# Memory query projection of a decoder step: from full products on column thirds to seven half-size products per pair of feature tiles

## The chip, the core and the metric

The kernel runs on one core of one Trainium2 chip. The metric is the time of one execution on the device, in microseconds (us); lower is better. The profile is that of one execution. Engines are named as in the profile: PE is TensorE's matmul, PEld its weight load, DVE is VectorE, ACT is ScalarE, POOL is GpSimd, SP is SyncE, which here issues DMAs.

## What is computed

One layer of a decoder for 1024 prompt tokens and 8 sample tokens, all in float32, with an output projection, attention into 256 memory tokens and an MLP. The part that matters here, from the reference:

```python
xp = xp + merge_groups(oa, o_r, gr, ...) @ w_out[l]
mk_p, mv_p = mem_kv(mem_prompt, norm_mem_kv[l], w_mk[l], w_mv[l])
xp = xp + mem_attend(rmsnorm(xp, norm_mem_q[l]), mk_p, mv_p, w_mq[l], w_mo[l])
xp = xp + sq_relu_mlp(rmsnorm(xp, norm_mlp[l]), w_up[l], w_down[l])

def mem_attend(h, mk, mv, w_mq, w_mo):
    q = (h @ w_mq).reshape(B, T, H_M, DH_M)          # 1024 x 1024 weights, 4 heads of 256
    s = jnp.einsum('bthd,bmhd->bhtm', q, mk) * DH_M ** -0.5
    p = jax.nn.softmax(s, axis=-1)
    o = jnp.einsum('bhtm,bmhd->bthd', p, mv).reshape(B, T, D_MODEL)
    return o @ w_mo
```

`rmsnorm` multiplies a token's row by one factor, `rsqrt(mean(x*x) + eps)`, and each feature by a gain. The sample tokens go through the same projections and attend to cached memory keys and values (`cmk`, `cmv`).

## The kernel before

Activations are kept transposed: 8 feature tiles of 128 partitions, with T = 1032 token columns (1024 prompt, 8 sample). CH is a third of them (344), HALF is 516, QC is 258. Each float32 operand of a large product is split into a high part of type fp32r (a copy on ACT) and the rest (a subtraction on DVE); a product is then three matmuls per 128-row step: high x high, high x low, low x high. `UH` and `UL` hold the two parts of the right operand, the rings `wh` and `wl` (4 buffers each) those of the weights, and `raw` (3 buffers) the weights as loaded.

The order of instructions comes from a planner that puts each engine's instructions in the order in which they would be ready by its own estimate, the earlier in the program first. Three things override it: `pin[0] = True` holds matmuls in program order, `tc.issue_after(ins)` puts a block's instructions behind `ins` on its engine, and `behind("Activation", "DVE")` does so for the latest instruction of both engines. Every engine, and SP's DMA queue, then runs its list strictly in order. A tile's tag names a buffer that tiles of the same tag share; a new tile waits until an older one is released.

The stages around the change:

1. Output projection (`proj_residual`, matmuls `pr_o`): per feature tile `ft` and column third `c`, first thirds 0 and 1 of all tiles, then third 2. `store` adds the residual into the tiles `x2[ft]`, squares them on ACT and adds the squares on POOL. `rstd_bcast` sums the squares by matmuls (`rs`), sends the row to a column and back through DRAM (power on POOL in `rsqrt_small`) and broadcasts it into `rb2`. Then eight DMAs write `x2` to `X2` in DRAM.
2. `split_gain` (L131) multiplies `x2` by the gain and splits it into `UH`/`UL`, columns 0 to 687 first, then the last third.
3. Query projection (`mq`, L1632 to L1661): for each of 4 pairs of feature tiles, 2 tiles x 3 thirds, each one accumulation of 8 x 3 matmuls of 344 columns. The eviction (L1652) multiplies by `rb2` and -1/16 into `qm`; its 8 sample columns go to `qdm` (POOL). After pairs 1 and 3, `dec_scores` replicates the sample queries (`rep_rows`) and multiplies them with the cached keys, loaded as `cmk` in 512 KB pieces: three of four on DVE (L1625), every fourth on POOL with a DVE reduction (L1619, L1620). The operands of the memory tokens (`mh`, `ml`) and their norm factor are prepared at the head of this stage.
4. Memory keys and values: `mem_keys_now(0)` (`mk`), two blocks of `mv`, `mem_keys_now(1)`, outputs to DRAM and back for `head_kv(0)`.
5. Attention: a pinned loop of 16 turns (4 heads x 4 token blocks). Turn by turn `scores` (`ms`, minimum L1764, exponential with scale -1 L1768, reciprocal, multiplication), `weights` (transposes, split), `values` (`mpv`, L1803/L1804 into `UH`/`UL`). `head_q` splits a head's queries, its low part on POOL (L1747). The rest of `mk` fills the gaps.
6. The memory output projection (`pr_m`), the up projection (L2106) and the down projection (L2271). The latter two already use the seven-product scheme with 258-column matmuls.

Of the kernel before, what the change touches and what calls it, by code (L numbers as in the profile page):

```python
# [19 lines left out]
P = 128  # L20
D = 1024
# [27 lines left out]
def decoder_step(ctx: ExitStack, tc: tile.TileContext, i: dict, o: dict):  # L49
# [764 lines left out]
    def dec_softmax(A, dt, SC, nt, c, nm):  # L814
# [7 lines left out]
        m3 = A.tile([P, 8, 16], F32, tag="dex", name=f"dm3_{nm}", bufs=2)[:c]  # L822
# [14 lines left out]
    def rep_rows(A, dt, src, nf, dst, nm, b0=0):  # L837

        for b in range(b0, b0 + nf // 4):
            tp = dt(f"rep_{nm}_{b}")  # L840
            for x in range(4):
                ex = A.tile([P, 8, 16], F32, tag="dex", name=f"dex_{nm}_{b}_{x}", bufs=2)
                nc.vector.tensor_copy(ex, src[:, 4 * b + x, :].unsqueeze(2).to_broadcast([P, 8, 16]))
                nc.tensor.transpose(tp[:, x * P : x * P + P], ex.rearrange("p s g -> p (s g)"), ident)
# [556 lines left out]
    def proj_residual(A, bank, base, ktorder, xsrc, xdst, ssum, nm, us0, steps, when, parts, ahead=0, early=None, stage=()):  # L1401
# [16 lines left out]
        def store(ps, ft, c):  # L1418
# [54 lines left out]
    def rstd_bcast(A, PS, bufs, ssum, last, r, dst, nm, rtag):  # L1473
# [9 lines left out]
        col = A.tile([86, 12], F32, tag="rcol", name=f"rcol_{nm}")  # L1483
        nc.sync.dma_start(col, row)
        rc = A.tile([86, 12], F32, tag="rrc", name=f"rrc_{nm}")
        rsqrt_small(rc, col, 12, 1.0 / D, 86)
        nc.sync.dma_start(rrow[r : r + 1, :].rearrange("a (p c) -> p (a c)", p=86), rc)
        nc.sync.dma_start(dst, bcast_rows(rrow[r : r + 1, :], P, T))

    with pool("x2") as XP:  # L1490
        x2 = [XP.tile([P, T], F32, tag=f"x2_{ft}", name=f"x2_{ft}") for ft in range(8)]
        g_mq = XP.tile([P, 8], F32, tag="g_mq", name="g_mq")
        nc.sync.dma_start(g_mq, i["g_mq"])
        with pool("c") as A:
            def decode_values():
                def dt(name):
                    return PB.tile([P, 512], F32, tag="av", name=name, bufs=1)

                acc = A.tile([P, T], F32, tag="dacc", name="dacc")
                for k in range(8):  # L1500
                    raw = A.tile([P, 1024], F32, tag="draw", name=f"cv_{k}", bufs=4)
                    gather(raw, i["cache_v"], idx, k)
                    with tc.issue_after(seen["DVE"]):
                        for x in range(8):
                            c = slice(x * P, x * P + P)
                            w = at[:, x % 4, 2 * k + x // 4 : 2 * k + x // 4 + 1]
                            if k == 0:
                                nc.vector.tensor_scalar(acc[:, c], raw[:, c], w, None, ALU.mult)
                            else:
                                nc.vector.scalar_tensor_tensor(acc[:, c], raw[:, c], w, acc[:, c], ALU.mult, ALU.add)  # L1510
                    yield
                vp = dt("vrep")
                mm(vp, selg, vdec, True, True)
                pd = A.tile([P, 1024], F32, tag="draw", name="pdv_8", bufs=4)
                nc.vector.tensor_mul(
                    pd[:, :512].rearrange("p (a v) -> p a v", v=P), vp.rearrange("p (a v) -> p a v", v=P),
                    at[:, :, 16:17].to_broadcast([P, 4, P]),
                )
                nc.vector.tensor_add(acc[:, :512], acc[:, :512], pd[:, :512])
                yield  # L1520

                with tc.issue_after(seen["PE"]):
                    op = dt("dop")
                    mm(op[:8, :], selgt, acc[:, 0:512], True, False)
# [44 lines left out]
    with pool("d") as A:  # L1569
# [62 lines left out]
        for pr in range(4):  # L1632
# [6 lines left out]
            for f, c in late + rest if pr else rest + late:  # L1639
# [15 lines left out]
                if (f, c) == (1, 2) and pr % 2:  # L1655
                    for _ in dec:
                        pass
# [932 lines left out]
```

## Time and profile before

| | |
|---|---|
| median of 3 runs | 1518.12 us (1514.62 to 1518.33) |
| the profiled execution | 1516.72 us, its span 1515.0 us |
| granted TensorE clock | 0.996 |
| PE busy | 1483.5 us (98%) |
| DVE, ACT, POOL busy | 1121.2 us (74%), 669.3 us (44%), 423.6 us (28%) |
| HBM | 150 GB/s over the span |

A matmul's recorded duration covers its way through the array, so records of neighbours overlap; the pace of matmuls is read from starts or from the merged chain. Records on DVE overlap a little too. A line number can be that of a helper: L75 is `mm`, L118 the low half in `unit_of`, L134 the low half in `split_gain`.

### The profile page before, as it was taken

The numbers are of one execution on the slowest core, as the hardware profiler recorded it, in microseconds if no ns is written. First come the engines' busy times: TensorE is split into PE (matmuls) and PEld (weight loads), VectorE is DVE, ScalarE is ACT, GpSimd is POOL, SyncE is SP. The second block draws the span as 40 slices with busy tenths as digits, with TensorE's granted clock in tenths as the row PEclk, the third lists the DMA queues.
The fourth block names the chain that finished last, engine by engine and source line by source line (L and its number), as shares of the span: only waits on it lengthen the run. The fifth ranks groups of instructions, "written<-read, shape, count | busy, mean of one in ns | idle before, by whom it ended". The sixth has DMA issues, their size and how long they took to land.

```text
span 1515.0 us, 27770 instructions
## 1 busy us (share of the span) xinstructions
PE 1483.5 (98%) x10909; PEld 1406.3 (93%) x10909; DVE 1121.2 (74%) x2200; ACT 669.3 (44%) x1314; POOL 423.6 (28%) x441
## 2 busy tenths in 40 slices
PE   9999999999999999999999999999999999999997
PEld 7899779998669999989999999999999999999997
DVE  7656536888766735557786988888889889787885
ACT  7433435666552432047535633333334444333454
POOL 0035323124313321125132223443335202020360
PEclk9999999999999999999999999999999999999999
DMA  8155727214847157362492433343335784536213
GB/s 292 56 186 187 185 58 186 70 35 138 248 140 268 56 194 191 120 200 86 152 323 71 145 129 134 140 154 140 141 142 169 258 285 125 183 86 193 87 43 112
DMA packets 120860, 231.39 MB, mean 153 GB/s; under 512 B 13216, under 2 KB 72661, under 8 KB 120602
## 3 DMA queue, kind: packets, MB, share of 16 engines
q1 hardware_dynamic: 89008, 170.50, 35.4%
q0 software_dynamic: 20592, 39.53, 8.4%
q10 hardware_dynamic: 11130, 19.60, 3.4%
q8 instruction: 85, 1.39, 0.4%
q14 instruction: 45, 0.37, 0.1%
HBM read 170.24 MB, written 57.52 MB: 150 GB/s over the span
## 4 chain that ended last, share of the span: by engine, by line
PE 77%; DVE 11%; DMA 5%; issue 3%; ACT 3%; POOL 1%; SPq 0%; DVEq 0%; ACTq 0%; POOLq 0%
PE dn L2271 17%; PE Z L2106 7%; PE qkp L75 6%; PE pr_o L75 6%; PE mq L75 5%; PE Y L2106 5%; PE pr_m L75 4%; PE X L2106 4%; PE grp L75 3%; PE sp L75 2%; PE av L75 2%; DVE wu L1921 1%; PE mpv L75 1%; DMA raw_up<-in_wall 1%; PE vap_z L511 1%
## 5 line engine op out<-in xcount | busy, mean ns | idle before, releaser
L2271 PE MATMUL dn<-UH,wd 128*128 128x258 f32 x1792 | 324.5, 283 | 1.8 <-DVE c L2375 1.3
L2271 PEld LDWEIGHTS dn<-UH,wd 128*128 128x128 f32 x1792 | 277.4, 189 | 2.5 <-ACT wd L2249 0.8
L2271 PE MATMUL dn<-UL,wd 128*128 128x258 f32 x896 | 252.8, 282 | 0.0
L2271 PEld LDWEIGHTS dn<-UL,wd 128*128 128x128 f32 x896 | 169.0, 189 | 0.0
L2132 ACT ACTIVATE hq<-r 128x258 f32<-128x258 f32 x128 | 53.7, 420 | 161.5 <-DVE r L2131 161.5
L2375 DVE TENSOR_TENSOR c<-c,dn 128x258 f32<-128x258 f32 x216 | 88.4, 418 | 32.6 <-PE dn L2271 31.1
L2106 PE MATMUL Z<-T_h,wu 128*128 128x258 f32 x512 | 99.8, 286 | 4.7 <-DVE u L2160 3.3
L1921 DVE TENSOR_TENSOR wu<-raw_up,wu 128x512 fp32r<-128x512 f32 x96 | 93.1, 971 | 9.7 <-ACT wu L1920 9.6
L2106 PE MATMUL X<-UH,wu 128*128 128x258 f32 x512 | 97.5, 282 | 0.0
L2249 ACT CAST wd<-raw_d 128x512 fp32r<-128x512 f32 x96 | 58.6, 618 | 77.1 <-PE dn L2271 72.2
L2106 PEld LDWEIGHTS Z<-T_h,wu 128*128 128x128 f32 x512 | 81.6, 189 | 6.4 <-DVE u L2160 4.1
L2242 ACT CAST UH<-raw_h 128x1032 fp32r<-128x1032 f32 x56 | 58.7, 1055 | 58.1 <-PE dn L2271 27.7
L2250 DVE TENSOR_TENSOR wd<-raw_d,wd 128x512 fp32r<-128x512 f32 x96 | 75.2, 789 | 11.5 <-ACT wd L2249 11.3
L2243 DVE TENSOR_TENSOR UL<-raw_h,UH 128x1032 fp32r<-128x1032 f32 x56 | 76.8, 1371 | 9.0 <-ACT UH L2242 8.9
L2106 PEld LDWEIGHTS X<-UH,wu 128*128 128x128 f32 x512 | 81.3, 188 | 0.2 <-ACT p L2157 0.2
L2139 POOL TENSOR_TENSOR ht<-hq 128x258 f32<-128x258 f32 x31 | 20.6, 663 | 195.6 <-ACT hq L2132 195.3
L117 ACT CAST wh_u<-raw_u 128x1024 fp32r<-128x1024 f32 x43 | 44.4, 1047 | 64.8 <-PE mq L75 42.9
L2263 POOL TENSOR_TENSOR raw_d<-raw_d,raw_d 128x512 f32<-128x512 f32 x16 | 22.1, 1378 | 181.0 <-DVE raw_d L2259 130.3
L2106 PE MATMUL Z<-T_l,wu 128*128 128x258 f32 x256 | 72.5, 283 | 0.0
L2106 PE MATMUL X<-UL,wu 128*128 128x258 f32 x256 | 72.2, 282 | 0.0
L1920 ACT CAST wu<-raw_up 128x512 fp32r<-128x512 f32 x96 | 57.2, 611 | 27.2 <-DVE raw_up L1927 24.1
L118 DVE TENSOR_TENSOR wl_u<-raw_u,wh_u 128x1024 fp32r<-128x1024 f32 x39 | 49.5, 1277 | 19.0 <-ACT wh_u L117 18.9
(595 smaller groups left out, 4808.9 us busy)
## 6 DMA issues: line engine op xcount, KB each, us to landing
raw_u<-in_wall SPq DMA_DIRECT2D x49, 512.0 KB
HT<-ht POOLq DMA_DIRECT2D x32, 516.0 KB
raw_h<-HT SPq DMA_DIRECT2D x32, 516.0 KB
raw_up<-in_wall SPq DMA_DIRECT2D x32, 512.0 KB
raw_d<-in_wall SPq DMA_DIRECT2D x32, 512.0 KB
HQ<-hq ACTq DMA_DIRECT2D x32, 387.0 KB
raw_h<-HQ SPq DMA_DIRECT2D x24, 516.0 KB
cmk<-in_cmk SPq DMA_DIRECT2D x16, 512.0 KB
```

Of the source, the lines that this page charges most:

```text
L75: pinned(nc.tensor.matmul(out, l, r, start=start, stop=stop))
L118: (lo_engine or nc.vector).tensor_sub(wl[:, :n], raw[:, :n], wh[:, :n].bitcast(F32))
L1920: nc.scalar.copy(w[:, :512], src)
L1921: nc.vector.tensor_sub(w[:, 512:], src, w[:, :512].bitcast(F32))
L2106: pinned(nc.tensor.matmul(ps, l, r[:, k, :], start=first and k == 0 and x == 0, stop=k == 3 and x == 2, skip_group_check=True))
L2132: nc.scalar.activation(h[:, PLACE[quad], :], r, AF.Square)
L2242: nc.scalar.copy(h, rv)
L2243: nc.vector.tensor_sub(l, rv, h.bitcast(F32))
L2249: nc.scalar.copy(w[:, :512], src)
L2250: nc.vector.tensor_sub(w[:, 512:], src, w[:, :512].bitcast(F32))
L2271: pinned(nc.tensor.matmul(ps, l, r[:, k, cq], start=first and k == 0 and x == 0, stop=k == 3 and x == 2, skip_group_check=True))
L2375: nc.vector.tensor_add(y, y, ps)
```

## The change

- **The product.** The 1024 x 1024 weights are seen as four pairs of 128-column tiles, and the features and the tokens are halved: a 2 x 2 by 2 x 2 block product, done with seven products of half size (numbered 1 to 7) and sums of blocks before and after. Products 1 and 2 (`first_columns`) run for pairs 0 and 1, then for pairs 2 and 3; then `other_columns` does products 6, 5, 7, 4, 3 of one pair after the other (6, 7, 4, 5, 3 for pair 0). All matmuls of the stage are pinned and have 258 columns. The weights are stored tile by tile (`_unit128`); each unit is loaded twice, once for products 1 and 2 (`WA`) and once for the sums (`q_loads`, `q_operands`).
- **The right operands.** Only the first half of the columns is split by `split_gain`. `early_sums`, `late_sums` and `last_sums` form the sums of `x2` blocks in place and split them into `T3`, `UH` and `UL`. `X2` is therefore written from inside `store`, in two pieces per feature tile, and third 2 of the output projection runs in the order 0, 4, 1, 5, 2, 6, 3, 7.
- **The norm factor.** Evictions are plain copies (ACT) and additions (DVE). The factor, as a column per token block (`fq`, through DRAM), becomes the scale of the exponential, and the maximum is multiplied by `nfq` for its bias. `rb2` is used for the sample columns alone.
- **Around it.** The `cmk` rows are loaded in 32 pieces of 256 KB into the tags `mph`/`mpl`, with bufs 2 each, which the `p1` tiles use too; all are reduced on DVE. The first half runs in pairs 2 and 3, the second in the `mv` stage. The loads of the memory tokens move to pairs 2 and 3. `x2`'s buffers stay alive through attention and hold `head_q`'s tiles; `head_q` of heads 2 and 3 is put behind the latest `mph` copy on ACT.

```diff
 # proj_residual
+            if c:
+                xs = slice(0, 2 * CH) if c == 1 else cs
+                nc.sync.dma_start(X2[ft, :, xs], xdst(ft)[:, xs])
-        order = [(ft, c) for ft in range(8) for c in range(2)] + [(ft, 2) for ft in range(8)]
+        order = [(ft, c) for ft in range(8) for c in range(2)] + [(ft, 2) for ft in KT_PAIRS]
...
-        for lo, hi in ((0, 2 * CH), (2 * CH, T)):
-            for kt in range(8):
-                split_gain(x2[kt][:, lo:hi], g_mq, kt, lo, hi)
+    for kt in range(8):
+        split_gain(x2[kt][:, :HALF], g_mq, kt, 0, HALF)
...
         def dec_scores(half):
...
+            for n in range(18):
+                if n < 16:
+                    raws[n] = A.tile([P, HALF], F32, tag=("mph", "mpl")[n % 2], name=f"cmk_{half}_{n}", bufs=2)
+                    nc.sync.dma_start(raws[n][:, :512], i["cmk"][:, n, ch])
+                if n < 2:
+                    continue
+                k = n - 2
+                with seq():
+                    for x in range(2):
+                        nc.vector.tensor_tensor_reduce(...)
                 yield
...
+        def early_sums(k):
+            x, z = x2[k], x2[k + 4]
+            nc.scalar.activation(x[:, hi_t], x[:, hi_t], AF.Copy, scale=g1)
+            nc.vector.scalar_tensor_tensor(x[:, lo_t], x[:, lo_t], g1, x[:, hi_t], ALU.mult, ALU.subtract)
+            nc.vector.scalar_tensor_tensor(x[:, hi_t], z[:, hi_t], g2, x[:, hi_t], ALU.mult, ALU.subtract)
+            nc.scalar.copy(T3[0][:, k, :], x[:, hi_t])
+            nc.vector.tensor_sub(T3[1][:, k, :], x[:, hi_t], T3[0][:, k, :].bitcast(F32))
...
+        def q_product(kind, pr, q, c, w, first):
+            if first:
+                banks_q[kind, pr, c] = PS.tile([P, 512], F32, tag="acc", name=f"mq_{kind}_{pr}_{c}", bufs=6)[:, :QC]
+            for k in range(4):
+                for x, (l, r) in enumerate(((wk, rh), (wk, rl), (wkl, rh))):
+                    pinned(nc.tensor.matmul(ps, l, r[:, k0 + k, tk], ...))
...
+        def q_operands(pr):
+            with seq():
+                nc.vector.tensor_sub(s3, a11, a21)
+            yield
+            # likewise: a21 += a22; a11 = a21 - a11; split 6, 7, 5, 4; a12 -= a11 and split 3
...
+        def other_columns(pr, order):
+            for n, q in enumerate(order):
+                for c in range(2):
+                    ps = q_product("z" if q in (6, 7, 4) else "y", pr, q, c, WB[pr][q], q in (6, 5))
+                    with seq():
+                        if q == 6:
+                            nc.vector.tensor_add(u2[:, cq], ps, p1[pr][:, cq])
+                        elif q == 7:
+                            nc.vector.tensor_add(u3[:, cq], ps, p1[pr][:, cq])
+                            if c in y5:
+                                nc.vector.tensor_add(f1[:, ch], y5[c], u3[:, cq])
+                        elif q == 4:
+                            nc.vector.tensor_add(f1[:, cq], ps, p1[pr][:, cq])
+                        elif q == 3:
+                            nc.vector.tensor_add(f0[:, ch], ps, u2[:, cq])
...
+                    yield
...
+        for k in range(3):
+            early_sums(k)
+        WA = {pr: unit(U_MQ + 2 * pr) for pr in range(4)}
+        with tc.issue_after(seen["rs"]):
+            early_sums(3)
+        q_loads(0)
+        late = late_sums()
+        next(late)
+        first_columns((0, 1), late)
+        with seq():
+            finish_rb2()
+        first_columns((2, 3), chain(late, q_operands(0)))
+        sums = chain(last_sums(0), last_sums(4))
+        next(sums)
         for pr in range(4):
+            cols = other_columns(pr, (6, 5, 7, 4, 3) if pr else (6, 7, 4, 5, 3))
+            if pr < 3:
+                q_loads(pr + 1)
+                work = chain(sums, q_operands(pr + 1)) if pr == 0 else q_operands(pr + 1)
+            if pr == 2:
+                mem_sums()
+                dec = dec_scores(0)
+            for n, _ in enumerate(cols):
+                if n > 1 or pr == 0:
+                    next(work, None)
...
+                if pr == 3 and n == 6:
+                    mem_operands()
+                if n > 1 and pr > 1:
+                    next(dec, None)
...
+        dec = chain(dec, dec_scores(1))
         mem_keys_now(0)
         for b in range(2):
...
+            for _ in range(10):
+                next(dec, None)
...
-            nc.vector.tensor_reduce(mn, sp, AX.X, ALU.min)
+            nc.vector.tensor_reduce(mn, sp, AX.X, ALU.max)
+            nc.vector.tensor_mul(mn, mn, nfq[:, 2 * tp : 2 * tp + 2])
...
-                nc.scalar.activation(sp[:, x, :], sp[:, x, :], AF.Exp, bias=mn[:, x : x + 1], scale=-1.0,
-                                     accum_out=sm[:, x : x + 1])
+                nc.scalar.activation(sp[:, x, :], sp[:, x, :], AF.Exp, bias=mn[:, x : x + 1],
+                                     scale=fq[:, 2 * tp + x : 2 * tp + x + 1], accum_out=sm[:, x : x + 1])
```

More of the change, by code (lines that the diff above doesn't have):

```diff
@@ L1600, in decoder_step @@
+        p1 = {pr: A.tile([P, HALF], F32, tag=("mph", "mpl")[pr % 2], name=f"p1_{pr}", bufs=2) for pr in range(2)}
+        T3 = [A.tile([P, 4, HALF], F32R, tag=f"t3{x}", name=f"t3_{x}") for x in "hl"]
+        m_h, m_l = [], []
         rm = A.tile([P, 2], F32, tag="rm", name="rm")
-        rsqrt_small(rm, sm2, 2, 1.0 / D)
-        nc.sync.dma_start(rrow[1:2, :256].rearrange("a (t p) -> p (a t)", p=P), rm)
         rmb = A.tile([P, 256], F32, tag="rmb", name="rmb")
-        nc.sync.dma_start(rmb, bcast_rows(rrow[1:2, :], P, 256))
+        spare = [0]
```

424 lines of the change are left out of this document (263 added, 161 removed).

## The prediction

> **What bounds the kernel now.** I read the page first: engine totals and the chain of work that ended last.
>
> ```profile
> PE 1483.5 (98%) x10909; PEld 1406.3 (93%) x10909; DVE 1121.2 (74%) x2200; ACT 669.3 (44%) x1314; POOL 423.6 (28%) x441
> ...
> PE 77%; DVE 11%; DMA 5%; issue 3%; ACT 3%; POOL 1%; SPq 0%; DVEq 0%; ACTq 0%; POOLq 0%
> PE dn L2271 17%; PE Z L2106 7%; PE qkp L75 6%; PE pr_o L75 6%; PE mq L75 5%; PE Y L2106 5%; PE pr_m L75 4%; PE X L2106 4%; PE grp L75 3%; PE sp L75 2%; PE av L75 2%; DVE wu L1921 1%; PE mpv L75 1%; DMA raw_up<-in_wall 1%; PE vap_z L511 1%
> ```
>
> TensorE bounds the kernel, and the changed projection (`mq`) is 5% of the chain. Averages over stages mislead, so the next view is busy time by stage. Columns: the stretch, its length, then busy us of PE, PEld, DVE, ACT and POOL, the granted clock, the DMA share and GB/s. Rows: the end of the output projection, the query projection, memory keys and values, memory attention, and a piece of the up projection.
>
> ```profile
> 516.00:547.70 31.70, 31.66 (x187) 27.43 (x185) 18.34 (x31) 14.30 (x28) 8.13 (x8) 1.00 0.55 192
> 547.70:639.80 92.10, 92.10 (x587) 91.47 (x587) 42.96 (x140) 16.16 (x24) 12.86 (x14) 1.00 0.55 156
> 639.80:673.70 33.90, 33.81 (x192) 29.23 (x192) 20.44 (x24) 13.08 (x15) 10.21 (x4) 1.00 0.56 184
> 673.70:750.60 76.90, 72.47 (x592) 69.66 (x590) 56.54 (x115) 51.15 (x119) 24.46 (x11) 1.00 0.34 106
> 905.00:945.00 40.00, 40.00 (x333) 39.76 (x332) 33.45 (x58) 14.93 (x34) 15.58 (x20) 1.00 0.40 144
> ```
>
> In the query stage PE has no idle time at the full granted clock, and VectorE works 42.96 of 92.10 us (47%). The up projection already uses seven products on 258-column matmuls; there VectorE stands at 33.45 of 40 us (84%) and PE still does not wait. Attention idles PE for 76.90 - 72.47 = 4.4 us.
>
> **The matmuls.** Removed are 8 feature tiles x 3 column chunks x 8 k-tiles x 3 terms = 576 matmuls of 344 columns; added are 4 pairs x 7 products x 2 chunks x 4 k-tiles x 3 terms = 672 of 258 columns. The mean durations of the groups overlap, so the pace comes from the chain in order of time, which merges back-to-back work (start, length, what, count):
>
> ```profile
> 547.77 30.34 PE mq L75 x192
> ...
> 579.55 44.48 PE mq L75 x283
> ```
> ```profile
> 924.96 2.87 PE Y L2106 x24
> 927.83 2.87 PE X L2106 x24
> 930.70 2.88 PE Z L2106 x24
> ```
>
> 30.34/192 = 0.1580 us at 344 columns, 2.87/24 = 0.1196 us at 258. Before: 576 x 0.1580 = 91.0 us. After: 672 x 0.1196 = 80.4 us. **Gain 10.6 us**, if nothing makes PE wait. From the two paces a matmul costs 0.000447 us per column and a fixed 0.0044 us, so the 96 additional ones cost 0.4 us, which is contained in the pace.
>
> The Trainium skill, "TensorE: Matmul & The Clock Gate", section "Back-to-back issue gap", speaks against this change: in streams of weight load and matmul it gives about 81 ns at 128 columns and about 131 ns at 512, a large fixed part. Interpolated (an estimate from that page) that is 109 ns at 344 and 98 ns at 258: 62.8 us before, 65.9 us after, a loss of 3.1 us. The trace disagrees: 158.0 against 119.6 ns, in proportion to the columns.
>
> **The norm factor.** The 24 multiplying evictions (L1652) go, and with them the wait for the broadcast row.
>
> ```profile
> DVE qm L1652 <- DMA rb<-rrow: 8.6, 1, 8.6
> ```
> ```profile
> L1652 DVE SCALAR_TENSOR_TENSOR qm<-mq,rb 128x344 f32<-128x344 f32 x24 | 12.2, 512 | 21.6 <-PE mq L75 13.0 <-DMA rb<-rrow 8.6
> L118 DVE TENSOR_TENSOR wl_u<-raw_u,wh_u 128x1024 fp32r<-128x1024 f32 x22 | 28.9, 1319 | 11.8 <-ACT wh_u L117 11.8
> L1625 DVE CUSTOM_DVE_ANT_0 cmk<-cmk,qrm 128x256 f32<-128x256 f32 x48 | 19.0, 458 | 3.1 <-ACT qrm L845 2.1 <-DMA cmk<-in_cmk 0.9
> L1685 DVE TENSOR_TENSOR wl_kv<-raw_kv,wh_kv 128x512 fp32r<-128x512 f32 x3 | 2.1, 690 | 1.9 <-ACT wh_kv L1684 1.9
> L1591 DVE SCALAR_TENSOR_TENSOR ml<-memT,g_mkv,mh 128x256 fp32r<-128x256 f32 x8 | 3.3, 481 | 3.1 <-ACT mh L1590 3.1
> ```
> ```profile
> L2375 DVE TENSOR_TENSOR c<-c,dn 128x258 f32<-128x258 f32 x216 | 88.4, 418 | 32.6 <-PE dn L2271 31.1
> ```
>
> VectorE waited 8.6 us for the row, PE not at all, so removing that wait is worth nothing. `finish_rb2` now sits behind the first eight products; its row is next read for `qdm` at the end of pair 0, 18 products of 12 x 0.1196 = 1.44 us later. In attention each of the 16 turns gets a [128x2] multiply between the maximum and the exponential. The nearest row is the reciprocal of that shape, 0.162 us:
>
> ```profile
> L1770 DVE RECIPROCAL msm<-msm 128x2 f32<-128x2 f32 x13 | 2.1, 162 | 2.8 <-ACT ms L1768 2.8
> ```
>
> Upper end 16 x 0.162 = 2.6 us, since VectorE works 56.54 of 76.90 us there and its results release transposes. The lower end is a gain of up to the 4.4 us that PE idles there, because `head_q` of heads 2 and 3 is reordered and its POOL work moved. I take **1.0 us lost**: the multiply is certain, the other not.
>
> **VectorE in the query stage.** From the rows above, inside the new stage: `late_sums` 16, `early_sums(3)` 3, `last_sums` 8 and `q_operands` 36 instructions of 512 or 516 columns, 63 x 0.690 = 43.5 us; evictions 10 per pair and two more in pairs 1 to 3, 46 x 0.418 = 19.2; 15 decode rows of two halves, 30 x 0.458 = 13.7; `mem_operands` 8 x 0.481 = 3.8; low halves of two `WA` units and of about four key/value units ahead, 6 x 1.319 = 7.9; some 1 us for `rep_rows`. Together 89 us against PE's 80.4. But records of neighbours overlap. The chain shows it:
>
> ```profile
> 626.13 0.42 DVE cmk L1625
> 626.56 0.01 DVE SCm L1625
> 626.57 0.34 DVE cmk L1625
> ```
>
> The second of two equal instructions adds 0.01 + 0.34 = 0.35 us, not 0.42. At 0.07 us less for each of some 160 instructions, 78 us remain, 97% of 80.4. VectorE thus goes from 47% to nearly full, above the 84% of the up stage. The `seq()` blocks fix the order on ACT and VectorE, so an eviction stands behind operand splits and decode rows, and behind the eviction the next product into the same bank. Cover: pairs 1 to 3 run 6, 5, 7, 4, 3, so most banks have two products (2.87 us) in between, and six banks exist. Ends: no loss (78 us fits), or 89 - 80.4 = 8.6 us. I take **2.5 us**, nearer to the overlapped pace, since in the 84% stage nothing was lost. The first products need only `WA[0]` and the low half of `UH`, whose split falls beside the last output products; a second load of every query unit (2 MB) finds a queue at 156 GB/s.
>
> **What moves.** X2's eight stores after `rb2` become sixteen pieces inside the output projection, ahead of the `WA` loads on SP's queue. `memn` and `memT` move from the head of the stage to pairs 2 and 3. POOL loses four multiplies. The 8 MB of `cmk` become 32 loads of 256 KB, half of them now in the keys/values stage. That stage moved 184 GB/s x 33.9 us = 6.2 MB; plus 4.2 MB is 308 GB/s, and the share 0.56 rises to 0.94. VectorE there: 20.44 + 32 x 0.35 + 1 = 32.6 of 33.9 us. Both fit just. Ends: nothing, or one late transfer at the longest landing in the chain:
>
> ```profile
> 627.63 3.73 DMA cmk<-in_cmk
> ...
> 655.43 5.05 DMA raw_u<-in_wall
> ...
> 662.82 5.66 DMA out_mv<-mvo
> ...
> 674.76 2.09 DMA out_mv<-mvo
> ```
>
> 5.7 us is the upper end; I take **1.5 us**, because PE was busy 33.81 of the 33.90 us there, so the present load costs it nothing.
>
> **Sum:** 10.6 - 1.0 - 2.5 - 1.5 = 5.6 us. The profiled execution took 1516.72 us (span 1515.0 plus 1.7 around it), which would become 1511.1; it stands 1.4 us below the median 1518.12 of runs from 1514.62 to 1518.33. On the median: **1512.5 us**, 0.37% less.
>
> **Rivals.**
> VectorE becomes the bound: the stage lasts the 89 us of its records instead of 80.4. For it: 97% and a fixed order. Against: the records overlap. Then 10.6 - 8.6 - 1.5 - 1.0 = -0.5, 1518.6 us: no change. Chance 0.22.
>
> The change keeps all: VectorE and DMA hide everything, 10.6 us, 1507.5 us; with idle time of attention taken too, 1505.5 or less. Chance 0.17.
>
> Slower: the decode rows wait for their loads, in order, in front of evictions. The `cmk` buffers share tags `mph`/`mpl` with `p1`, whose second tiles stay in use until product 4 of pairs 2 and 3. With one free buffer per tag, row k+2's load starts when row k is done. In between VectorE has two evictions, two splits and one row, 2 x (0.418 + 0.690) + 2 x 0.458 = 3.1 us. A landing beyond 3.1 us stops VectorE for the excess at every second row: at 5.05 us 1.92 x 7.5 = 14.4 us in place of the 2.5, so 10.6 - 14.4 - 2.5 = -6.3, **1524.4 us**. Slower by over 0.3% from a landing of 4.8 us. For: 5.05 and 5.66 in the trace at 0.56 share. Against: 2.09 for a transfer of 256 KB, and at step 4 of pair 2 no eviction is late yet. Chance 0.20.
>
> A matmul has a fixed part that eats the gain: for 672 small ones to cost as much as 576 large ones it would be 258 columns' worth, 0.115 us; the rows give 0.0044. Then 91.0 us stays and 5.0 is lost: 1523.1 us. Chance 0.01; the page named above would have it so.
>
> That the change does not do what it says cannot be for the matmul count, which follows from the loops; for the norm factor it is priced at nothing.
>
> **How the numbers follow.** A measurement of this kernel tells about 0.3% (4.6 us) from no change. My forecast's own band, 1509.5 to 1513.5, has 0.40, with the full gain 0.57 for faster; VectorE as the bound 0.22 for the same; the last two 0.21 for slower. The range 1505.5 to 1524.4 reaches from the full gain with attention's part to the decode rows at 5.05 us; outside are about 0.05 below and 0.10 above. Faster cases alone: 1505.5 to 1513.5.
>
> **What would show it.** Right: `mq` matmuls 672 at 0.120 us pace; query stage 82 to 84 us; VectorE around 90% in it; PE's waits there under 3 us in sum, on VectorE additions; keys/values stage near 300 GB/s. Wrong: VectorE idle before `cmk` rows with DMA as the releaser (the slower rival); VectorE without idle time and PE waiting over 8 us (the bound); pace above 0.13 us (the fixed part); attention longer than 78 us.

## The result and the profile after

The changed kernel takes 1537.33 us (median of 4 runs, 1533.87 to 1538.27) against 1516.37 us of the kernel before in the same comparison: ratio 1.0135, 95% interval 1.0109 to 1.0161, some 20 us slower. The forecast was 1512.5, the range ended at 1524.4. The profiled execution took 1533.87 us, its span is 1532.1 us.

The page of the changed kernel, engine totals and the chain's share:

```profile
PE 1483.8 (97%) x11005; PEld 1406.6 (92%) x11005; DVE 1176.4 (77%) x2330; ACT 693.6 (45%) x1362; POOL 409.3 (27%) x429
...
PE 42%; DVE 5%; issue 1%; DMA 1%; ACT 1%; DVEq 0%; ACTq 0%
```

TensorE's busy time is what it was (1483.5 before), although 10.6 us of matmuls were to go; VectorE's grew by 55 us. Stage by stage: the two rows run from the first `mq` matmul to the first score (query projection with memory keys and values), and from there to the first `pr_m` matmul (attention). First the kernel before, then the changed one; the columns are those of the stage view in the prediction.

```profile
547.70:673.80 126.10, 126.01 (x779) 120.78 (x778) 63.40 (x163) 29.34 (x39) 23.07 (x17) 1.00 0.55 164
673.80:739.50 65.70, 61.38 (x505) 59.32 (x504) 50.79 (x104) 46.36 (x110) 24.46 (x11) 1.00 0.29 90
```
```profile
550.20:681.10 130.90, 120.52 (x874) 114.72 (x874) 100.99 (x254) 54.73 (x94) 8.27 (x4) 0.96 0.51 161
681.10:761.20 80.10, 64.78 (x507) 62.37 (x506) 66.50 (x149) 46.77 (x105) 26.33 (x12) 0.94 0.33 107
```

The first stretch became 4.8 us longer instead of 10.6 shorter, attention 14.4 us longer. In both PE idles (10.4 and 15.3 us) and the granted clock is 0.96 and 0.94 instead of 1.00. Who is waited for, PE alone, from 500 to 800 us (total, times, longest):

```profile
PE mq_z L1705 <- DVE u L1785: 6.5, 2, 4.9
PE ms L75 <- DVE mko L1878: 4.7, 1, 4.7
PE mk L75 <- DVE wl_u L118: 4.4, 2, 2.3
PE mpv L75 <- DVE mmn L1960: 3.3, 1, 3.3
```

PE's busy time in the two rows together fell by only 2.1 us (187.4 to 185.3), not by 10.6, and its idle time grew by 21.3. The lower clock is the rest: the four slices of 10 us with the lowest clock (600 to 610 us at 0.66, shown below, and these three) lack 10.2 us of full speed, in part while PE was idle.

```profile
670.00:680.00 10.00, 7.68 (x46) 7.21 (x45) 7.12 (x27) 3.45 (x5) 0.00 (x0) 0.83 0.85 272
680.00:690.00 10.00, 5.33 (x35) 5.09 (x33) 7.04 (x32) 0.99 (x1) 1.17 (x1) 0.80 0.96 313
690.00:700.00 10.00, 7.91 (x51) 7.33 (x50) 9.40 (x19) 6.31 (x17) 1.20 (x1) 0.69 0.37 121
```

The long waits are all on VectorE, in three places. **In the query stage**, SP's queue, then VectorE in order of time:

```profile
SPq L1613 <- DMA rrow<-rm: 6.8, 1, 6.8
```
```profile
594.64 0.33 SPq L1613 DMA_DIRECT2D rmb<-rrow  x1
595.06 0.86 SPq L1730 DMA_DIRECT2D raw_mq<-in_wall  x2
```
```profile
601.28 0.69 DVE L1750 TENSOR_TENSOR s_q<-raw_mq,raw_mq 128x512 f32<-128x512 f32 x1 [7.75 <-DMA raw_mq<-in_wall]
602.00 0.69 DVE L1753 TENSOR_TENSOR raw_mq<-raw_mq 128x512 f32<-128x512 f32 x1
602.61 0.42 DVE L1785 TENSOR_TENSOR u<-mq_z,p 128x258 f32<-128x258 f32 x1
```
```profile
603.18 0.55 PE L1705 MATMUL mq_z<-UH,wq 128*128 128x258 f32 x1 [4.94 <-DVE u L1785]
```

SP stands until the memory tokens' norm factor has landed in DRAM and only then fetches pair 2's weights; VectorE stands 7.75 us for them with an eviction behind (L1785), and PE stands 4.94 us for that.

**In front of attention** the second half's decode rows run until 688.6 us, though the first scores began at 681.1 us. They wait for their loads, with the last key product's eviction (`mko`), `nfq` and the first maximum behind them in order:

```profile
685.89 0.43 DVE L1654 CUSTOM_DVE_ANT_0 cmk<-cmk,qrm 128x256 f32<-128x256 f32 x1 [2.93 <-DMA cmk<-in_cmk]
...
686.59 0.69 DVE L1878 TENSOR_TENSOR mko<-mk,rmb 128x512 f32<-128x512 f32 x1
...
688.25 0.43 DVE L1654 CUSTOM_DVE_ANT_0 cmk<-cmk,qrm 128x256 f32<-128x256 f32 x1
...
688.90 2.32 DVE L1921 TENSOR_SCALAR fq<-fq 128x8 f32<-128x8 f32 x1
691.14 0.68 DVE L1959 TENSOR_REDUCE mmn<-ms 128x2 f32<-128x512 f32 x1
```

**In attention** the new product of 256 numbers (L1960) is short or very long. Its group, then POOL's timeline and VectorE's beside it:

```profile
L1960 DVE TENSOR_TENSOR mmn<-mmn,nfq 128x2 f32<-128x2 f32 x16 | 8.8, 552 | 0.1
```
```profile
700.83 2.39 POOL L1942 TENSOR_TENSOR ql<-qm,qh 128x1024 fp32r<-128x1024 f32 x1 [9.63 <-PE ms L75]
...
712.26 4.71 POOL L1942 TENSOR_TENSOR ql<-qm,qh 128x1024 fp32r<-128x1024 f32 x2 [1.54 <-ACT qh L1941]
```
```profile
701.21 0.69 DVE L1959 TENSOR_REDUCE mmn<-ms 128x2 f32<-128x512 f32 x1
702.26 0.69 DVE L1981 TENSOR_TENSOR mpl<-mtr,mph 128x512 fp32r<-128x512 f32 x1 [0.36 <-ACT mph L1979]
702.87 0.37 DVE L1960 TENSOR_TENSOR mmn<-mmn,nfq 128x2 f32<-128x2 f32 x1
...
711.99 0.68 DVE L1981 TENSOR_TENSOR mpl<-mtr,mph 128x512 fp32r<-128x512 f32 x1
712.59 2.10 DVE L1960 TENSOR_TENSOR mmn<-mmn,nfq 128x2 f32<-128x2 f32 x1
714.61 0.15 DVE L826 COPY dm_m<-dtq_m 128x4 f32<-128x4 f32 x1
714.79 2.26 DVE L827 TENSOR_TENSOR SCm<-SCm,dm_m 128x64 f32<-128x64 f32 x1
716.97 0.68 DVE L1959 TENSOR_REDUCE mmn<-ms 128x2 f32<-128x512 f32 x1
```

16 x 0.15 would be 2.4 us; the group took 8.8. The product at 712.59 ends with the first of POOL's two `ql`, the subtraction at 714.79 with the second (POOL is done at 716.97). In each of the trace's five products longer than 0.3 us the end lies 0.02 us behind the end of a POOL instruction; the other eleven met none and took 0.13 to 0.16 us. The maximum at 701.21 and the split of `mtr` at 702.26, which read PSUM, take their usual 0.69 us although a `ql` runs from 700.83 to 703.22.

So three theories, one for each place: **A**, the weights behind the slow small transfer; **B**, VectorE held by POOL at operations whose operands all lie in SBUF; **C**, the decode rows in front of attention. The common rival is the prediction's: VectorE is simply full. From 550 to 640 us it was busy 67.7 of 90 us (75%), so in the query stage the rival does not hold.

### The profile page after: what moved, and what is told of

It is laid out like the page before. It is cut to its first block, busy times and chain, and to the rows that moved or that the text cites. A ratio compares the mean times of both kernels' runs of the same rounds, so it can differ in the third digit from the quotient of the medians.

```text
span 1532.1 us, 28202 instructions
## 1 busy us (share of the span) xinstructions
PE 1483.8 (97%) x11005; PEld 1406.6 (92%) x11005; DVE 1176.4 (77%) x2330; ACT 693.6 (45%) x1362; POOL 409.3 (27%) x429
## 4 chain that ended last, share of the span: by engine, by line
PE 42%; DVE 5%; issue 1%; DMA 1%; ACT 1%; DVEq 0%; ACTq 0%
PE dn L2470 17%; PE Z L2305 9%; PE Y L2305 6%; PE X L2305 6%; PE pr_m L75 4%; DVE UL L2442 1%; DVE wd L2449 1%; DVE c L2574 0%; DMA raw_h<-HQ 0%; DMA raw_h<-HT 0%; DVE c L2579 0%; DVE T_l L2139 0%; DVE c L2503 0%; DVE UL L2139 0%; DVE xs L2274 0%
## 5 line engine op out<-in xcount | busy, mean ns | idle before, releaser
L75 PE MATMUL qkp<-UH,wh_u 128*128 128x344 f32 x192 | 63.1, 329 | 0.1
L75 PE MATMUL qkp<-UH,wl_u 128*128 128x344 f32 x192 | 62.5, 326 | 0.0
```

The costliest lines, as they stand in the source:

```text
L75: pinned(nc.tensor.matmul(out, l, r, start=start, stop=stop))
```

## The experiments

Beside the time, each trace gives two stretches: Q from the first `mq` matmul to the first score, M from there to the first `pr_m` matmul. Ratios are to the kernel before in the same comparison, whose median lay between 1512.25 and 1519.29 us.

| kernel | Q, us | M, us | ratio, 95% interval |
|---|---|---|---|
| before | 126.1 | 65.7 | 1 |
| changed | 130.9 | 80.1 | 1.0135 [1.0109, 1.0161] |
| e4: before, factor in the exponential | 125.8 | 72.2 | 1.0042 [1.0024, 1.0060] |
| h1: e4, product on ACT | 125.8 | 65.5 | 1.0002 [0.9987, 1.0017] |
| e2: changed, product on ACT | 131.2 | 76.9 | 1.0116 [1.0089, 1.0143] |
| e1: changed, memory tokens on POOL's queue | 128.3 | 83.9 | 1.0135 [1.0101, 1.0168] |
| e3: changed, cmk on POOL's queue | 142.8 | 71.5 | 1.0143 [1.0112, 1.0173] |
| f1: changed, scatter early | 122.0 | 84.1 | 1.0138 [1.0106, 1.0169] |
| f2: f1, product and scaling of `fq`, `nfq` on ACT | 123.6 | 77.2 | 1.0102 [1.0078, 1.0127] |
| j2: changed, row in two packets | 124.1 | 86.6 | 1.0125 [1.0095, 1.0155] |
| j3: j2, product and scaling on ACT | 126.0 | 79.5 | 1.0054 [1.0035, 1.0073] |
| c1: changed, half 1 left out | 128.6 | 70.9 | 1.0045 [1.0018, 1.0071] |
| c2: changed, half 1 loads only | 132.8 | 76.8 | 1.0111 [1.0079, 1.0142] |
| g0: changed, six rows in attention | 130.5 | 83.5 | 1.0164 [1.0140, 1.0188] |
| g1: g0, other scatter place, product and scaling on ACT | 135.0 | 79.9 | 1.0149 [1.0125, 1.0172] |
| j4: j3, rows spread | 136.6 | 65.0 | 1.0066 [1.0049, 1.0084] |
| i1: f2 without half 1 | 122.9 | 66.0 | 0.9999 [0.9981, 1.0018] |
| j1: j3 without any row | 117.7 | 66.0 | 0.9944 [0.9928, 0.9960] |

**B, the small product (e4, h1, e2).** e4 puts only the norm factor's move into the kernel before:

```diff
-                nc.vector.scalar_tensor_tensor(q[:, cs], ps[:, :CH], -1.0 / 16.0, rb2[:, cs], ALU.mult, ALU.mult)
+                nc.vector.tensor_copy(q[:, cs], ps[:, :CH])
...
-            nc.vector.tensor_reduce(mn, sp, AX.X, ALU.min)
+            nc.vector.tensor_reduce(mn, sp, AX.X, ALU.max)
+            nc.vector.tensor_mul(mn, mn, nfq[:, 2 * tp : 2 * tp + 2])
```

> The kernel before with only the norm factor moved: plain evictions, maximum times nfq (128x2, VectorE), exponential with scale fq. Theory B: the 16 small products wait for POOL's ql wherever the two meet: attention 77 to 82-86 us, the run 4 to 9 us slower than the kernel before (1520 to 1525). Rival, the product costs only its own 0.15 us: 16 x 0.15 = 2.4 us at most, the run 0 to 2.5 us slower, and all of attention's loss in the changed kernel comes from its late start.

Slower by 0.42%, 6.4 us, all of it in M. Of e4's trace, the product's group and two of its three longest beside two `ql` of POOL:

```profile
L1771 DVE TENSOR_TENSOR mmn<-mmn,nfq 128x2 f32<-128x2 f32 x16 | 10.2, 639 | 0.1
```
```profile
708.08 2.40 POOL L1753 TENSOR_TENSOR ql<-qm,qh 128x1024 fp32r<-128x1024 f32 x1 [1.84 <-ACT qh L1752]
...
714.18 2.40 POOL L1753 TENSOR_TENSOR ql<-qm,qh 128x1024 fp32r<-128x1024 f32 x1
```
```profile
708.24 2.25 DVE L1771 TENSOR_TENSOR mmn<-mmn,nfq 128x2 f32<-128x2 f32 x1
714.21 2.39 DVE L1771 TENSOR_TENSOR mmn<-mmn,nfq 128x2 f32<-128x2 f32 x1
```

h1 is e4 with that product on ACT, and nothing else changed:

```diff
-            nc.vector.tensor_mul(mn, mn, nfq[:, 2 * tp : 2 * tp + 2])
+            for x in range(2):
+                nc.scalar.activation(mn[:, x : x + 1], mn[:, x : x + 1], AF.Copy, scale=nfq[:, 2 * tp + x : 2 * tp + x + 1])
```

> The kernel before with the norm factor in the exponential and the product of maximum and nfq on ACT. Theory B (VectorE held by POOL, not the product's own time): of the 6.4 us that the same move cost with the product on VectorE, 3 to 6 us come back: 1517 to 1521. Rival, the longer chain maximum, product, exponential is what costs: no change against the product on VectorE (1523), or slower, as ACT's two instructions take longer than VectorE's one.

The loss is gone, within an interval of 0.15%, although ACT spends three times the 2.4 us:

```profile
L1772 ACT ACTIVATE mmn<-mmn,nfq 128x1 f32<-128x1 f32 x32 | 7.8, 289 | 3.3 <-DVE mmn L1770 3.2
```

So B is shown: neither the longer chain nor the product's own time costs anything that can be measured here, VectorE's wait for POOL does. In the changed kernel the same edit (e2) brings 0.2%, which its interval doesn't tell from nothing. The likely reason, which no run isolates, is that M begins late there because of the decode rows:

> The changed kernel with the 128x2 product of maximum and nfq on ACT (two 128x1 copies with a scale per partition) instead of VectorE. Theory B: on VectorE that product has two SBUF sources and stands until POOL's running ql is done (0.15 us alone, 2.10, 1.94, 2.03 us beside ql); 3 to 4 such stalls plus the clock after them cost attention 5 to 9 us. Then attention goes from 91 us to 82 to 86 and the run is 5 to 9 us faster than the changed kernel, although ACT gets 32 more instructions. Rival C, attention is late because the decode rows run until 688.6 us: PE stalls at 712 and 742 us stay whatever engine multiplies, gain below 2 us, or a loss of up to 5 us because ACT's fixed time sits on the path of each turn.

**A, the query stage (e1, f1, j2).** e1 issues the six transfers of the memory tokens from POOL's queue (`nc.sync.dma_start` becomes `nc.gpsimd.dma_start` at `memn`, `memT`, `rrow` and `rmb`).

> The changed kernel with the loads of the memory tokens and their norm factor (memn, memT, rrow<-rm, rmb<-rrow: 6 DMAs) issued from POOL's queue instead of SP's. Theory A (head of line on SP): in the changed kernel SP stood 6.8 us at rmb<-rrow in front of pair 2's weight loads, VectorE then stood 7.75 us for raw_mq, PE 4.94 us for the eviction behind it at 603 us, and the clock fell to 0.66 in that 10 us. Then pair 2's weights come some 7 us earlier, that PE stall goes, and the run is 4 to 8 us faster than the changed kernel (1529 to 1533). Rival 1, VectorE is simply full in the query stage: under 1.5 us gained. Rival 2, the cmk loads that wait for p1's buffers on the same queue hold the weights as well: the stall only moves to pair 3, 0 to 3 us gained.

No gain; the theory in its first form fell. VectorE still waited 6.68 us for `raw_mq`. The loads were issued at once, but landed after 8.7 us, while 54 packets under 512 bytes were under way (e1's transfers from 584 to 594 us in 40 slices; the first row is the busy share of the DMA engines in tenths, the second GB/s):

```profile
DMA  6996785420000930630000150099000038049115
GB/s 246 295 311 246 263 312 197 181 99 17 0 0 0 115 115 0 16 66 0 0 0 0 16 49 0 33 147 82 16 33 16 16 66 33 33 66 66 16 16 115
DMA packets 252, 0.82 MB, mean 82 GB/s; under 512 B 54, under 2 KB 54, under 8 KB 251
...
raw_mq<-in_wall SPq DMA_DIRECT2D x2, 512.0 KB, 8.7
```

`rrow<-rm` writes 256 single numbers of 4 bytes. Between short bursts the DMA engines stand idle in these rows, so as far as the records go the weights don't wait for bandwidth; the 0.6 to 0.9 in f1's expectation holds for the bursts alone. f1 moves the transfer, with the `memn` loads, ahead of the stage's weights:

```diff
-                raw = spare_row(f"memn_{x}", 6)
+                raw = G.tile([P, T], F32, tag="raw", name=f"memn_{x}", bufs=3)
...
+        mem_sums()
         WA = {pr: unit(U_MQ + 2 * pr) for pr in range(4)}
```

> The changed kernel with the memory tokens' sums (memn loads into raw buffers, squares, rrow<-rm) ahead of the stage's weight loads, as in the kernel before, and only the read of rmb behind them. Theory A, second form: taking the six DMAs off SP's queue gained nothing (VectorE still stood 6.68 us for raw_mq), because rrow<-rm, 256 packets of 4 bytes, is in flight for 7 to 8 us and in that time the DMA engines were 0.6 to 0.9 busy at 16 to 66 GB/s, so the weights come late from any queue. With the scatter gone from mid-stage pair 2's weights land before 592 us, VectorE's wait of 7.75 us and PE's stall of 4.94 us go, the clock stays at 1.0: 5 to 8 us faster than the changed kernel (1529 to 1532). Rival, the four 512 KB loads and the buffers are the limit, not the scatter: the wait shrinks by 2 us at most, under 2 us gained. Rival, what is gained here is lost again in front of attention, where the loads bound: under 2 us gained, query stage shorter by 5.

j2 leaves everything in its place and only writes the row in two packets of 512 bytes, behind the weights:

```diff
-            nc.sync.dma_start(rrow[1:2, :256].rearrange("a (t p) -> p (a t)", p=P), rm)
+            transpose(tp[:2, :P], rm, ident)
+            nc.scalar.copy(rmt, tp[:2, :P])
+            nc.sync.dma_start(rrow[1:2, :256].rearrange("a (t p) -> (a t) p", p=P), rmt)
```

> The changed kernel with only the way of the memory tokens' norm factor changed: the [128x2] column is transposed on PE, copied on ACT and written to DRAM as 2 rows of 512 bytes instead of 256 pieces of 4 bytes, behind pair 2's weight loads. The loads of memn and memT stay where they are. Theory A, second form (the slow scatter holds the weights): pair 2's weights land some 7 us earlier, PE's stall of 4.9 us and the slow clock behind it go, first mq to first mk falls from 86.5 to about 80 us, without f1's longer gap behind the statistics (5.9 instead of 3.0 us). In all 3 to 6 us faster than the changed kernel if this reaches attention, 0 to 2 us if the second half's loads in front of attention take it back. Rival (it was the place of the memn loads, which f1 moved as well): the stall stays, 86 us.

In both the stall of 4.94 us is gone (in j2 one of 2.3 us, also before `mq_z`, is left). The stretch from 600 to 610 us, in the changed kernel, then in f1:

```profile
600.00:610.00 10.00, 6.82 (x41) 6.85 (x42) 6.52 (x13) 2.18 (x4) 0.00 (x0) 0.66 0.18 70
```
```profile
600.00:610.00 10.00, 10.00 (x86) 10.00 (x85) 7.97 (x19) 2.81 (x5) 0.00 (x0) 1.00 0.36 87
```

and Q falls by 8.9 (f1) and 6.8 us (j2). But M grows by 4.0 and 6.5 us, f1's place of the transfer costs PE 2.4 us ahead of Q (a wait for `rrow` on ACT, 0.4 us in the changed kernel), and the ratios stay at 1.0138 and 1.0125. (j2's traced run was the slowest of its four, 1543.18 us against a median of 1537.42, so its M may be long.) That was f1's second rival. So this transfer in mid-stage makes the stall, but removing it alone gains nothing that can be told from the noise of about 6 us: most of the gain is lost again in front of attention and in it. Whether its many small packets or its place in SP's order delay the weights stays open. e1 speaks for the packets, since there the weights were issued at once and still came late; j2 does not separate the two, because its row also stands behind the weights.

**C, the second half's rows (c1, c2, e3, g0, j4).** c1 leaves out the loads and products of half 1, c2 only the products.

> The changed kernel without the second half of the decode rows: 16 cmk loads (4.2 MB) and their 32 products on VectorE are left out, one copy fills the place. Theory C: these rows between 650 and 688.6 us hold the evictions and the start of attention: PE's idle time from 670 to 700 (9 us, and the clock at 0.69 to 0.83) goes, 9 to 14 us faster than the changed kernel (1523 to 1528). Rival, attention is late because of POOL's hold and the query stage alone: under 4 us.

> The changed kernel with the second half's 16 cmk loads kept and their 32 products on VectorE replaced by 16 copies of 128x2 (the products are left out). If VectorE's work is what is too much in front of attention (11 us of products), it gains nearly what the run without loads gains, over 8 us. If the loads' bandwidth and order are (share 0.85 to 0.96 at 272 to 313 GB/s from 670 to 690), it gains under 4 us.

c1 gains 0.90% (1.0135 to 1.0045), 13.6 us; c2 0.24%, 3.6 us, which its interval doesn't tell from nothing. So the second half costs 13.6 us (some 8 to 19 by the two intervals), and about 10 of them (4 to 16) come with the 4.2 MB that are loaded in front of attention, not with VectorE's arithmetic. Whether the loads cost by their bandwidth or by their place in the order is not separated by this. c2's VectorE from 644 to 700 us shows what is left, the same wait:

```profile
DVE SCm L1653 <- DMA cmk<-in_cmk: 6.9, 4, 4.0
```

Three attempts to keep the work and change its place failed. e3 issues the `cmk` loads from POOL's queue:

> The changed kernel with its 32 cmk loads issued from POOL's queue instead of SP's. Theory A+C: the loads wait in order on SP for a buffer (24.2 us in all before L1646 on p1's release, 9.4 on rows) and hold back weight loads, and are held back by weight loads; apart from each other, the query stage loses its 4.9 us PE stall and the decode rows end before 682 instead of 688.6: 5 to 10 us faster than the changed kernel. Rival, DMA bandwidth at a share of 0.85 to 0.96 bounds the stretch 670 to 690: the rows still end near 688 and at most the query stage's 3 to 5 us are gained. Rival, POOL's ql stands behind waiting loads: attention starts later and it is slower by 2 to 6 us.

Q became 11.9 us longer and M 8.6 shorter: the loss moved. g0 moves rows behind the first scores (six of the eight that were expected run there in its trace, from 690.93 to 698.31 us):

> The changed kernel with the last eight decode rows' place in the order moved behind the first scores of attention; the last key product and its eviction, the split of head 0's keys and the first maximum stand ahead of them. Theory C, order: the second half's loads and rows are not too many in themselves but stand, in order, ahead of what attention needs; PE's 4.7 us before the first scores (for mko) and the clock of 0.69 to 0.83 from 670 to 700 go: 6 to 10 us faster than the changed kernel. Rival, bandwidth: the weights of the last key products share 313 GB/s with the rows wherever these stand: under 3 us. Rival, VectorE's 11 us of products only move into attention, where the same PE waits for it: under 2 us.

It was 0.3% slower than the changed kernel, within the noise, and nothing was gained. The rows met POOL's `ql` in attention, and one of them was held as in B:

```profile
695.14 2.55 DVE L1654 CUSTOM_DVE_ANT_0 cmk<-cmk,qrm 128x256 f32<-128x256 f32 x1
```

g1 added the other repairs to g0, with the scatter at yet another place:

> All that the runs pointed to, in one: the late rows, the memory tokens' sums behind the statistics' last row copy (memn in the buffer that the queries' rows use later), maximum times nfq on ACT, fq and nfq scaled on ACT at pair 2. If the three losses add: query stage 80 us (79.8 measured with the scatter early), attention near 70 us, up projection as in the changed kernel: 1537 - 7 - 5 - 8 = 1513 to 1521, about the kernel before or a little faster. If the load bandwidth in front of attention takes back what the query stage gains: 1523 to 1530.

That place was bad: PE stood 6.4 us at `mq_x` for a copy behind the squares of `memn` on ACT. It tells nothing of the sum.

**Together (f2, j3, j4, i1, j1).**

> f1 with the product of maximum and nfq on ACT and the scaling of fq and nfq on ACT at pair 2. If the query stage's scatter and POOL's hold on VectorE's small products are two separate losses, they add: 5 to 8 us of f1 and 3 to 5 us (3.0 measured for the product alone, 2.3 for fq's own wait at 688.9): 1524 to 1529, still 0.5 to 0.9% slower than before because the decode rows in front of attention remain. If the first only moves work against the bound in front of attention: 1531 to 1534.

f2 took 1529.55 us, between the two forecasts; its gain over f1, 0.36%, is hardly more than the noise.

> j2 with maximum times nfq on ACT and fq, nfq scaled there at pair 2: 1525 to 1529 (f2 had 1529.6 with a gap of 5.9 us at the start of the stage, which this one doesn't have). If the gains don't add: 1530 to 1534.

j3 is the best version of the change that leaves nothing out: 1527.37 us, 1.0054, 0.8% better than the changed kernel. So the repairs of A and B, which brought 0.1% (j2) and 0.2% (e2) alone, bring 0.8% together. That this is more than their sum is likely, not shown: the intervals nearly touch, and j3 also scales `fq` and `nfq` on ACT, which neither j2 nor e2 does (the scaling of `fq` took VectorE 2.32 us in the changed kernel). j4 spreads the rows over the `mv` products:

```diff
-            us = [unit(U_MV + 4 * b + x) for x in range(4)]
+            us = []
             for kp in range(4):
+                us.append(unit(U_MV + 4 * b + kp))
+                for _ in range(3 if (b, kp) in ((0, 0), (0, 1), (1, 3)) else 2):
+                    next(dec, None)
```

> j3 with the second half's rows spread over the weight units of the mv products (two or three rows behind each unit's low half) instead of ten in a row behind each block of four units. In j3 neither VectorE (5.67 of 10 us) nor the DMA engines (0.79) were full from 670 to 680 and PE worked 4.48 of 10 us: ten rows in a row ask for 256 KB every 0.70 us, 366 GB/s, more than the 313 GB/s seen, and wait one by one. Spread, they are done before the last key products: PE's 7.6 us before the first scores go, 5 to 9 us faster than j3: ratio to before 0.999 to 1.003. Rival, the loads' sum bounds (weights and rows, 11 MB in 41 us): the stall moves into the mv products, 0 to 3 us: 1.004 to 1.006.

The rival held. M became 65.0 us, as short as before, and Q 136.6: the time was lost a stage earlier, at the replicated sample queries and in the `mv` products.

```profile
PE rep_m L844 <- DVE dex_m L843: 3.7, 1, 3.7
PE mv L75 <- ACT wh_u L117: 3.7, 1, 3.7
```

Without half 1 (i1), and then without any row (j1; the 32 loads and 64 products are left out):

> f2 (scatter early, maximum times nfq on ACT) without the second half of the decode rows (16 loads and 32 products left out, one copy in their place): all three losses removed at once, to see what the seven products leave over. If the account is complete: projection with keys and values about 122 us from its first matmul to the first score (126.1 before), attention 66 to 68 us (65.7 before), 0 to 8 us below the kernel before, ratio 0.995 to 1.000, although this run has 11 us of VectorE's work and 4.2 MB less to do than before. If a fourth loss exists: 1.003 to 1.008. If it comes out below 0.995, the losses hid more than the 10.6 us of the matmuls.

> j3 with both halves of the decode rows left out (32 loads, 8.4 MB, and 64 products on VectorE; one copy per half in their place): what of the matmuls' 10.6 us is left when VectorE and the loads have nothing else. If VectorE's fullness and the loads are the rest: first mq to first score 114 to 117 us (80.4 + 33.9 is 114.3; 122.9 with the first half's rows), attention 66 to 68, ratio 0.991 to 0.995. If a stall of another kind remains: 120 us or more, ratio 0.997 or above.

i1 equals the kernel before: its Q is 3.2 us shorter, and f1's place of the scatter costs 2.8 us ahead of Q (PE waits for `rrow` on ACT). j1 is the first that wins, by 0.56% (0.40 to 0.72), as expected (Q is 0.7 us over the expected 117). In its two stages the granted clock is 1.00, and PE idles 2.0 and 4.9 us:

```profile
551.70:669.40 117.70, 115.70 (x876) 111.13 (x875) 85.01 (x150) 57.61 (x99) 10.77 (x5) 1.00 0.41 129
669.40:735.40 66.00, 61.09 (x506) 59.55 (x504) 50.40 (x103) 49.00 (x135) 23.98 (x11) 1.00 0.29 87
...
590.00:630.00 40.00, 40.00 (x336) 39.97 (x335) 28.37 (x66) 10.71 (x18) 0.00 (x0) 1.00 0.39 121
```

Q is 8.4 us below before's 126.1, and 0.56% of 1519 us is 8.5. The seven products do save most of what was counted. (j1 has less to do than the kernel before; the kernel before was not run without its rows, but PE was busy 126.01 of 126.10 us there, so they cost its Q at most 0.1 us of idle time.) None of the three other arrangements of the decode rows that were tried was free; before, they ran beside a VectorE that was 47% busy.

## Why the prediction was wrong, point by point

The sum forecast 10.6 us of gain and 5.0 us of losses. Measured were 20.5 us more (1.35% of 1516.37), so the losses came to about 31 us. All three terms of loss were too small.

- **The matmuls: right.** 336 records in 40 us are 0.119 us each (counting one or two cut at the edges), 0.1196 was predicted. j1 keeps 8.4 of the 10.6 us. The rival of a fixed part that eats the gain did not come true.
- **"What moves": the step that failed most.** It was priced at 1.5 us with an upper end of 5.7; c1 measured 13.6 for the second half of the rows. Its reason was that PE was busy 33.81 of 33.90 us there, so that the present load cost nothing; that says nothing of a load that is two thirds larger. The step added 4.2 MB to the keys/values stage, found 308 GB/s and a share of 0.94, and said that both fit just. The changed kernel did show that load:

```profile
650.00:660.00 10.00, 10.00 (x46) 7.87 (x45) 8.75 (x25) 2.10 (x2) 0.00 (x0) 1.00 0.93 308
```

But a stage mean that just fits does not mean that every load is in time: the rows queue with the weights, wait, and have the first maximum of attention behind them on VectorE. It was also more than 4.2 MB: part of the first half did not fit into pairs 2 and 3, and 20 of the 32 loads (5.2 MB) were issued after 639 us. The bound of one late landing was wrong in kind: the rows stand in order behind their loads and add their lateness, here three waits of 2.22, 0.66 and 2.93 us, with the weights' low halves, `mko` and the first maximum behind them. PE waits for the first two of these (4.4 and 4.7 us) and then runs at a lower clock.
- **"The norm factor": mis-sized.** 1.0 us, upper end 2.6 = 16 x 0.162, from a reciprocal of the same shape. Measured on the kernel before: 6.4 us, 10.2 us of VectorE for the 16 products. The reciprocal has one operand in SBUF, the product two: the right shape, the wrong operands. Before's trace did show the price, a decode row of 2.19 us at 639.11 and one `wl_kv` of attention, which takes 0.69 us elsewhere, beside a `ql` of POOL that ran from 715.05 us to 717.45:

```profile
715.96 2.05 DVE L1685 TENSOR_TENSOR wl_kv<-mko,wh_kv 128x512 fp32r<-128x512 f32 x1
```

It wasn't looked for.
- **"VectorE in the query stage": mis-sized, and for another reason.** 2.5 us were taken, the upper end was 8.6. Until the first `mk`, 86.5 us, 636 of the 672 query matmuls ran, which is 76.1 us at the predicted pace: about 10 us were lost. The largest stall was 4.9 us for `raw_mq`, with the slow clock behind it. The prediction saw `memn` and `memT` move to pairs 2 and 3 and did not count the two small transfers that go with them, nor that SP waits between them with weights queued behind. Repairing it alone did not shorten the run.
- **The rival on the slower side** had the right mechanism, rows in order behind their loads, at the wrong place: of VectorE's 7.5 us of waits for `cmk`, 1.7 lie in the query stage and 5.8 in front of attention. Its 1524.4 us was 13 us too low. The rival "VectorE becomes the bound" did not happen in the query stage, where VectorE was 75% busy, not 97%; in front of attention c2 removes 11 us of its work and gains 3.6.
- **"What would show it"** named the right signs: VectorE idle before `cmk` rows with DMA as the releaser, and attention longer than 78 us. (The prediction's 76.9 us for attention before reach 11 us into the next stage; M, which doesn't, is 65.7 before and 80.1 after, 14.4 us more.)
- The up projection was 4.6 us shorter in the changed kernel's profile than in before's (327.7 to 332.3 us from first `Z` to first `dn`). It can't be put down to the change: e4 and h1, which keep the full products, show 330.9 and 330.2 us, and the other runs of the changed kernel 328.9 to 333.6.

## What to carry to other kernels

A stage that makes PE's work shorter also makes the cover shorter for everything that ran beside it: ask where each displaced load and each displaced vector instruction goes, and price it there, with the queue that stands behind it, not by a mean share that "just fits". The price of a tiny vector instruction is that of its operands' place: with both in SBUF and GpSimd at work, it costs until GpSimd's instruction ends. When several repairs bring nothing alone, one loss may hide the other: try them together before giving any of them up, and leave the displaced work out once to see what the idea itself is worth.

## What the runs showed of the hardware

- VectorE instructions with two SBUF operands are held until the subtraction that POOL is running ends: [128x2] 0.15 us alone, 2.0 to 2.4 us beside a `ql` of 2.4 us; [128x64] 2.26; a decode row 2.55 instead of 0.42 (2.50 and 2.60 in the changed kernel, at 640.18 and 645.22 us). A one-operand scaling of 128x8 took 2.32 us beside a `ql` from 688.83 to 691.20, while its twin at 688.60, just ahead of that `ql`, took 0.17, and the reciprocal at 744.34 us took 0.15 us beside POOL's 744.04 to 746.42. Operations with an operand in PSUM were not held. The Trainium skill, "GPSIMD Engine Reference", section "8. Key points", says that GpSimd shares its SBUF interfaces with VectorE, with contention for instructions with two SBUF inputs or in a 2-port mode; the traces agree for two inputs, and the scaling of 128x8 may be the second case, which no run here tests.
- SP waited 6.8 us for a transfer of 256 single numbers of 4 bytes, 1 KB in all (POOL's queue 8.0 in e1). In e1 weights issued beside it on the other queue took 8.7 us, against 3.5 in the changed kernel (medians of `raw_mq`); that the small packets are the cause isn't separated.
- A stall of PE costs more than its length. After the 4.94 us at 603 us the granted clock was 0.66 in the slice, 41 matmuls in 6.82 us of PE, 0.166 us each. The length of the stall alone doesn't decide: after one of 3.3 us in attention (slice 710 to 720 us) the clock stayed at 1.00, but after one of 2.3 us (PE resumed with `mk` at 675.42 us) it was 0.83 in the slice, and matmuls started 0.21 us apart for the next 3 us instead of 0.12. The Trainium skill, "TensorE: Matmul & The Clock Gate", section "What's actually happening", puts the drop behind an idle window of about 3.4 us. The stalls of 4.94 and 3.3 us agree with it, the one of 2.3 us does not.
